# A hybrid diffusion block: norm statistics summed by a matrix of ones, and rsqrt over whole rows

## The chip, the cores and the metric

The kernel runs on one core of a Trainium2 chip. The metric is the time on the device of one execution, in microseconds; the time before is 2035.62 us, the median of three runs (2035.23 to 2038.11). The engines are TensorE (PE in the profile; PEld is its loading of weights), VectorE (DVE), ScalarE (ACT), GpSimd (POOL) and SyncE (SP), which issues the large loads.

## The reference, cut to what matters

Two streams of 256 tokens, latent and context, pass through two layers of width 1024. A layer is an FFN, a mixer of four branches, and a second FFN. Ahead of each stands an RMS norm with a scale and a shift per channel:

```
def rmsnorm(x, g):
    y = x * rsqrt(mean(x * x, axis=-1) + EPS)
    return y * g
h = rmsnorm(x, g) * (1 + mod[3 * slot + 1]) + mod[3 * slot]
x = x + 0.5 * mod[3 * slot + 2] * (silu(a) * b) @ w2      # FFN; the mixer is alike, with w_o
def layernorm(x, g, b):                                   # over 256 channels, in the conformer branch
    mu = mean(x); var = mean(square(x - mu))
    return (x - mu) * rsqrt(var + EPS) * g + b
```

The context stream ends with the second layer's keys and values, so from the second mixer on only the latent stream goes on. A last RMS norm stands at the end.

## The kernel before, in words

Activations lie with channels on the 128 partitions and tokens along the row: `xt` has eight tiles k of 128 channels, and 512 tokens, stream 0 in columns 0 to 255 and stream 1 in 256 to 511. Every main product is made of three matmuls, `mm3` (L215 to L217): the high and the low part of a weight times the high part of the input, and the high part of the weight times the low part of the input. A block of weights is loaded (`raw`), cast to `whi` on ScalarE (L199), and its rest `wlo` is made on VectorE (L200). Of `whi` and `wlo` there are six buffers each, of `raw` four; `spent` marks where a block's last matmul stands.

**The end of a stage.** `down` (called at the end of each FFN and mixer) makes the eight output tiles m. `residual` adds each to `xt` (L417, VectorE), and for the next norm its square is made on ScalarE (L409, or L406 for m = 0) and added to `acc` (L413). With two streams the last LAST = 2 tiles are made by stream: first the matmuls of stream 0 for both, over 256 columns, then `nxt.stat(0)`, then those of stream 1, `nxt.stat(1)`, then `nxt.apply(0)`. The next stage begins with `nxt.apply(1)` and a group of four units, whose matmuls over stream 0 run first, k by k through the four units, and then those over stream 1, unit by unit. This stands at four places: the first FFN, the first mixer, the second FFN and the third.

**The statistics.** `x_rstd(s)` sums squares over channels, which lie on partitions. `tok_stat` does it by matmuls that take `acc`, and the last tile's square apart, as weights and a column of ones as input (L258), one per 128 tokens; so the sums stand in a column, tokens on partitions. `rsqrt` is nine VectorE operations on 128x2 (L230 to L247). `tok_bcast` spreads the column over all partitions by transposes (L267) into PSUM (`aux`), from where `part` reads it: for each k a product z (L464, VectorE), the high part (L468, ScalarE) and the low part (L469, VectorE).

**The other users.** `conv` makes the layer norm of the conformer branch in the same way, once for the mean and once for the variance, over 512 tokens in the first mixer and 256 in the second; it is a generator, of which `tap` takes steps between matmuls. `LateNorm` serves the last FFN: the products are made without rstd, which is applied after them; its `late_stat` is called in the middle of the first group. `FinalNorm` is the last one.

**What sets the order.** Apart from the start of the kernel, the order on each engine is made by a planner that runs ahead of time: it takes the program's instructions, and picks for an engine among those that may run by their order in the program. Small tiles come from pools: tag s1 has HSLOT = 6 slots of 128x256 (the squares, z, the small DFT table of `fourier`, loaded at L811), tag s2 has 47 of 128x512, PSUM has four `mm` and four `aux`. A tile takes a slot where it is first written and gives it back after its last use.

Of the kernel before, what the change touches and what calls it, by code (L numbers as in the profile page):

```python
# [10 lines left out]
F32 = mybir.dt.float32  # L11
# [34 lines left out]
TAP_0 = (2, 1)  # L46
TAP_1 = (1, 3)

LAST = 2
HSLOT = 6  # L50
FREE = 2
NSLOT = 47
# [29 lines left out]
def hybrid_block(ctx: ExitStack, tc: tile.TileContext, a, out, dbg=None):  # L82
# [25 lines left out]
    def small(n, dt=F32, tag=None, bufs=6):  # L108
        return sm.tile([P, n], dt, tag=tag or f"sm{n}", name=nm("sm"), bufs=bufs)
# [30 lines left out]
    make_identity(nc, ident)  # L140
    ones_d = const.tile([P, 1], F32, name="ones_d")
    nc.vector.memset(ones_d, 1.0 / D)
    ones_c = const.tile([P, 1], F32, name="ones_c")
    nc.vector.memset(ones_c, 1.0 / 256)
    ones_w = const.tile([P, 63], F32, name="ones_w")
    nc.vector.memset(ones_w, 0.0)
    nc.vector.memset(ones_w[:, 31:32], 1.0)
# [13 lines left out]
    nc.scalar.activation(cw[:, :, 0:2], c_in, AF.Silu)  # L161


    ln_b_h = const.tile([P, DEPTH, 2], F32, name="ln_b_h")
    nc.gpsimd.tensor_scalar_mul(ln_b_h, ln_b, 0.5)
    dw_h = const.tile([P, DEPTH, 2, TAPS], F32, name="dw_h")
    nc.gpsimd.tensor_scalar_mul(dw_h, dw_w, 0.5)
    b_gate_h = const.tile([P, DEPTH, 4, KD], F32, name="b_gate_h")
    nc.gpsimd.tensor_scalar_mul(b_gate_h, b_gate, 0.5)

    rope_c = const.tile([P, S], F32, name="rope_c")
# [50 lines left out]
        nc.vector.tensor_tensor(out=lo[:, :n], in0=src, in1=hi[:, :n], op=ALU.subtract)  # L222
        return hi, lo

    def rsqrt(ps, n):

        h = small(n, tag=f"rh{n}")
        y = small(n, tag=f"rs{n}")
        t = small(n, tag=f"rt{n}")
        nc.vector.tensor_scalar(out=h, in0=ps, scalar1=0.5, scalar2=0.5 * EPS, op0=ALU.mult, op1=ALU.add)  # L230


        nc.vector.tensor_scalar(
            out=y.bitcast(I32), in0=h.bitcast(I32), scalar1=-0.5,
            scalar2=float(0x5F3759DF - 0x400000 - 2**31 + round(np.log2(RSQRT) * 2**23)), op0=ALU.mult, op1=ALU.add,
        )
        nc.vector.tensor_tensor(out=t, in0=y, in1=y, op=ALU.mult)
        nc.vector.tensor_tensor(out=t, in0=t, in1=h, op=ALU.mult)
        nc.vector.scalar_tensor_tensor(
            out=y, in0=t, scalar=1.5 * RSQRT**2, in1=y, op0=ALU.subtract, op1=ALU.mult  # L240
        )
        nc.vector.tensor_tensor(out=t, in0=y, in1=y, op=ALU.mult)
        nc.vector.tensor_tensor(out=t, in0=t, in1=h, op=ALU.mult)
        nc.vector.scalar_tensor_tensor(
            out=t, in0=t, scalar=5 / 3 * RSQRT**6, in1=t, op0=ALU.subtract, op1=ALU.mult
        )
        nc.vector.scalar_tensor_tensor(  # L247
            out=y, in0=t, scalar=1.25 * RSQRT**12, in1=y, op0=ALU.add, op1=ALU.mult
        )
        return y  # L250

    def tok_stat(srcs, ones, T):

# [10 lines left out]
    def tok_bcast(r, T):  # L264
        ps = paux()
        for j in range(T // P):
            nc.tensor.transpose(ps[:, j * P : (j + 1) * P], r[:, j : j + 1].to_broadcast([P, P]), ident)  # L267
        return ps
# [131 lines left out]

    last_square = {}

    def square_in(k, s):
        c = cols(s)
        if k == 0:
            nc.scalar.activation(acc[:, c], xt[:, k, c], AF.Square)  # L406
            return
        sq = s1()
        nc.scalar.activation(sq, xt[:, k, c], AF.Square)  # L409
        if k == KD - 1:  # L410
            last_square[s] = sq
            return
        nc.vector.tensor_tensor(out=acc[:, c], in0=acc[:, c], in1=sq, op=ALU.add)  # L413

    def residual(m, s, ps, G, sq):
        c = cols(s)
        nc.vector.scalar_tensor_tensor(  # L417
            out=xt[:, m, c], in0=ps[:, c], scalar=G[:, m, s : s + 1], in1=xt[:, m, c],
            op0=ALU.mult, op1=ALU.add,
        )  # L420
        if sq:
            square_in(m, s)

    def x_rstd(s, T=S):
        J = T // P
        ps = tok_stat([acc[:, s * S : s * S + T], last_square.pop(s)], ones_d, T)
        return tok_bcast(rsqrt(ps[:, :J], J), T)

    class Norm:

# [43 lines left out]
    class LateNorm(Norm):  # L474
# [6 lines left out]
            pass  # L481

        def late_stat(self):
            rstd = x_rstd(0)
            self.r = s2()
            nc.scalar.copy(self.r[:, :S], rstd[:, :S])

        def begin(self):
            Norm.begin(self)
# [73 lines left out]
    def down(blocks, parts, NB, G, last, nxt, group=1, filler=None):  # L563
# [12 lines left out]
        for g, count in starts:  # L576
# [12 lines left out]
            spent(*ws)  # L589
            for i, ps in enumerate(pss):  # L590
                for s in range(NB):
                    residual(g + i, s, ps, G, last)
                if last and NB == 1:
                    nxt.tile(g + i)
            if not last and filler:
# [76 lines left out]
    def mixer(l, NB, norm, nxt, filler):  # L672
# [75 lines left out]
        def conv():  # L748
# [14 lines left out]
                    )  # L763
                    yield

            J = T // P
            o = [keep.pop(("co", i)) for i in range(2)]
            tot = s2()
            nc.vector.tensor_tensor(out=tot[:, :T], in0=o[0][:, :T], in1=o[1][:, :T], op=ALU.add)
            yield  # L770
            ps = tok_stat([tot], ones_c, T)
            mu = small(J)
            nc.vector.tensor_copy(mu, ps[:, :J])
            yield
            mub = tok_bcast(mu, T)
            sq = []
            for i in range(2):
                nc.vector.tensor_tensor(out=o[i][:, :T], in0=o[i][:, :T], in1=mub[:, :T], op=ALU.subtract)
                q = s2()
                nc.scalar.activation(q[:, :T], o[i][:, :T], AF.Square)  # L780
                sq.append(q)
            nc.vector.tensor_tensor(out=sq[0][:, :T], in0=sq[0][:, :T], in1=sq[1][:, :T], op=ALU.add)
            yield
            ps = tok_stat([sq[0]], ones_c, T)
            r = rsqrt(ps[:, :J], J)
            yield
            rb = tok_bcast(r, T)
            for i in range(2):
                y, th = s2(), s2()
                nc.vector.scalar_tensor_tensor(  # L790
# [540 lines left out]
```

## Time and profile before

| | us |
|---|---|
| median of three runs | 2035.62 |
| the profiled execution | 2034.05 |
| its span | 2032.2 |
| PE busy | 1998.6 (98%) |
| DVE busy | 1325.8 (65%) |
| ACT busy | 731.9 (36%) |

The profile is of one execution; its span goes from the first to the last instruction of the program. Starts in a timeline are microseconds from the start of the span. Matmuls are pipelined: the time one takes on TensorE is the distance from its start to the next one's, and its length in the table is longer. A float32 matmul shows as two records. In square brackets stands the idle time of the engine ahead of a row, and what ended it.

### The profile page before, as it was taken

To read this page: it belongs to the slowest core of one execution; us is meant where nothing else is said; L and a number is where in the kernel's file an instruction comes from. 1 tells how busy PE (TensorE), PEld (TensorE's weight loads), DVE (VectorE), ACT (ScalarE), POOL (GpSimd) and SP (SyncE) were. 2 spreads that over 40 slices of the span, in tenths; PEclk is the share of its full clock that TensorE was granted. 3 is DMA by queue.
4 is the path that set the end of the run, shared out by engine and by line. 5 is a ranking of instruction groups with operands and counts; after the bars stand their busy time and mean duration, and the time that the engine had idled before them with its cause. 6 is when DMAs were issued, how large, how long until landed. Compare 5 with 4: busy or idle time off the path is not lost.

```text
span 2032.2 us, 28076 instructions
## 1 busy us (share of the span) xinstructions
PE 1998.6 (98%) x11074; PEld 1709.5 (84%) x11074; DVE 1325.8 (65%) x2338; ACT 731.9 (36%) x1142; POOL 5.1 (0%) x30
## 2 busy tenths in 40 slices
PE   6999999999999999999999999999999999999998
PEld 4888878888887778888888888888888999899998
DVE  5886697676756654689578455552424878777665
ACT  3322322333344442432222234222223545665443
POOL 0000000000000000000000000000000000000000
PEclk8999999999999999999999999999999999999999
DMA  7755466433221323266457432643333453446663
GB/s 284 243 177 188 149 207 188 148 96 99 73 83 57 109 73 94 74 206 200 150 179 241 152 125 85 197 139 90 112 88 102 145 161 120 140 152 201 182 182 94
DMA packets 83492, 294.08 MB, mean 145 GB/s; under 512 B 9504, under 2 KB 10144, under 8 KB 83360
## 3 DMA queue, kind: packets, MB, share of 16 engines
q1 hardware_dynamic: 82784, 291.54, 45.9%
q8 instruction: 87, 1.43, 0.3%
q10 hardware_dynamic: 576, 0.75, 0.1%
q14 instruction: 45, 0.37, 0.1%
HBM read 289.10 MB, written 1.05 MB: 143 GB/s over the span
## 4 chain that ended last, share of the span: by engine, by line
PE 96%; DVE 2%; ACT 1%; issue 0%; DMA 0%; DVEq 0%; ACTq 0%
PE mm L215 30%; PE mm L216 30%; PE mm L217 30%; PE aux L989 1%; PE aux L972 1%; PE aux L945 1%; PE aux L337 1%; PE aux L258 1%; PE aux L832 1%; PE aux L294 0%; PE aux L857 0%; PE aux L267 0%; PE aux L818 0%; DVE acc L1144 0%; DMA par<-in_par 0%
## 5 line engine op out<-in xcount | busy, mean ns | idle before, releaser
L215 PE MATMUL mm<-s,whi 128*128 128x512 f32 (+2 forms) x3354 | 1168.3, 349 | 2.3 <-ACT s L468 1.9
L216 PE MATMUL mm<-s,whi 128*128 128x512 f32 (+2 forms) x3354 | 1162.4, 347 | 2.1 <-DVE s L469 2.1
L217 PE MATMUL mm<-s,wlo 128*128 128x512 f32 (+2 forms) x3354 | 1162.3, 347 | 1.3 <-DVE wlo L200 1.3
L199 ACT CAST whi<-raw 128x1024 fp32r<-128x1024 f32 (+1 forms) x408 | 416.6, 1032 | 919.8 <-PE mm L216 698.5
L215 PEld LDWEIGHTS mm<-s,whi 128*128 128x128 f32 x3354 | 633.8, 189 | 96.3 <-issue 8.5
L217 PEld LDWEIGHTS mm<-s,wlo 128*128 128x128 f32 x3354 | 634.5, 189 | 80.4 <-DVE wlo L200 1.7
L216 PEld LDWEIGHTS mm<-s,whi 128*128 128x128 f32 x3354 | 635.0, 189 | 79.0 <-DVE s L469 3.1
L200 DVE TENSOR_TENSOR wlo<-raw,whi 128x1024 fp32r<-128x1024 f32 (+1 forms) x408 | 486.3, 1199 | 319.9 <-ACT whi L199 316.7
L358 DVE SCALAR_TENSOR_TENSOR s<-ada,cw,s 128x512 f32<-128x512 f32 x392 | 268.8, 745 | 48.2 <-DMA ada<-in_w_ada 48.0
L417 DVE SCALAR_TENSOR_TENSOR xt<-mm,modG,xt 128x256 f32<-128x256 f32 x192 | 84.5, 478 | 118.5 <-PE mm L217 118.0
L221 ACT CAST s<-s 128x512 fp32r<-128x512 f32 (+1 forms) x104 | 59.4, 571 | 85.4 <-DVE s L642 52.5
L760 DVE SCALAR_TENSOR_TENSOR s<-pad,dw_h,s 128x512 f32<-128x512 f32 (+1 forms) x120 | 73.8, 615 | 2.1
L222 DVE TENSOR_TENSOR s<-s,s 128x512 fp32r<-128x512 f32 (+1 forms) x104 | 64.8, 623 | 5.5 <-ACT s L221 5.5
L1060 ACT ACTIVATE s<-mm,b_gate_h 128x512 f32<-128x512 f32 (+1 forms) x64 | 35.4, 579 | 77.1 <-PE mm L217 76.7
L468 ACT ACTIVATE s<-s,mod 128x256 fp32r<-128x256 f32 x80 | 38.1, 504 | 37.9 <-DVE s L464 37.9
L1083 DVE SCALAR_TENSOR_TENSOR s<-s,mm 128x512 f32<-128x512 f32 x48 | 32.7, 682 | 27.6 <-PE mm L217 22.1
L642 DVE TENSOR_TENSOR s<-s,mm 128x512 f32<-128x512 f32 x66 | 44.9, 680 | 3.6 <-PE mm L217 3.5
L949 DVE TENSOR_REDUCE sm<-aux 128x1 f32<-128x512 f32 (+1 forms) x48 | 28.6, 595 | 26.3 <-PE aux L945 26.2
L957 ACT ACTIVATE s<-aux,sm,sm 128x512 f32<-128x512 f32 (+1 forms) x48 | 34.0, 708 | 29.2 <-DVE sm L952 29.2
L513 DVE TENSOR_TENSOR s<-mm,s 128x256 f32<-128x256 f32 x44 | 18.1, 420 | 36.2 <-PE mm L217 36.2
L632 ACT ACTIVATE s<-mm 128x512 f32<-128x512 f32 x66 | 38.9, 589 | 5.7 <-PE mm L217 5.7
L469 DVE SCALAR_TENSOR_TENSOR s<-s,mod,s 128x256 fp32r<-128x256 f32 x80 | 36.1, 478 | 1.5 <-ACT s L468 1.5
(134 smaller groups left out, 697.3 us busy)
## 6 DMA issues: line engine op xcount, KB each, us to landing
raw<-in_w SPq DMA_DIRECT2D x208, 512.0 KB, 4.4
ada<-in_w_ada SPq DMA_DIRECT2D x144, 512.0 KB, 3.9
raw<-in_w_in SPq DMA_DIRECT2D x100, 512.0 KB, 4.1
raw<-in_w SPq DMA_DIRECT2D x64, 448.0 KB, 4.0
raw<-in_w_br SPq DMA_DIRECT2D x20, 512.0 KB, 3.7
raw<-in_w_o SPq DMA_DIRECT2D x16, 512.0 KB, 4.4
xt<-in_xt SPq DMA_DIRECT2D x4, 512.0 KB, 6.1
s<-s SPq DMA_DIRECT2D x16, 128.0 KB, 2.2
```

The lines of the kernel that those rows point to most:

```text
L199: nc.scalar.copy(hi[:, :n], raw[:, :n]),
L200: nc.vector.tensor_tensor(out=lo[:, :n], in0=raw[:, :n], in1=hi[:, :n], op=ALU.subtract),
L215: nc.tensor.matmul(ps, lhsT=wh, rhs=xh, start=first, stop=False)
L216: nc.tensor.matmul(ps, lhsT=wh, rhs=xl, start=False, stop=False)
L217: nc.tensor.matmul(ps, lhsT=wl, rhs=xh, start=False, stop=last)
L221: nc.scalar.copy(hi[:, :n], src)
L222: nc.vector.tensor_tensor(out=lo[:, :n], in0=src, in1=hi[:, :n], op=ALU.subtract)
L358: nc.vector.scalar_tensor_tensor(out=t, in0=src, scalar=cs, in1=t, op0=ALU.mult, op1=ALU.add)
L417: nc.vector.scalar_tensor_tensor(out=xt[:, m, c], in0=ps[:, c], scalar=G[:, m, s : s + 1], in1=xt[:, m, c], op0=ALU.mult, op1=ALU.add,)
L632: nc.scalar.activation(s[:, :T], ps[:, :T], AF.Silu, bias=bias)
L642: nc.vector.tensor_tensor(out=h[:, :T], in0=s[:, :T], in1=ps[:, :T], op=ALU.mult)
L760: nc.vector.scalar_tensor_tensor(out=ov, in0=h[:, :NB, j : j + S], scalar=dw_h[:, l, i, j : j + 1], in1=ov, op0=ALU.mult, op1=ALU.add,)
```

## The change

Sums over partitions for the norms that are followed by another stage, and for the conformer's layer norm, are made by `sum_all`: one float32 matmul with a 128x128 matrix of 1 / D as weights and the squares (or values) as input, which leaves the sum in every partition. `rsqrt` then works on the whole 128x256 (128x512 in the first layer's conformer norm) instead of 128x2 or 128x4, and its result needs no spreading. Its scratch tiles h and t are taken from tag s1, the result y from a new tag `rstd` with two slots; in `conv` existing s2 tiles are used. The last tile's square is now added to `acc` like the others, save before the final norm, which keeps the old way. `LateNorm` uses the result without a copy. In `conv` the mean is subtracted with its factor in one operation, and the step for the copy of the mean is gone, so the generator has one step fewer. LAST becomes 3. `dw_w` and `b_gate` are halved in place, without tiles of their own.

```diff
--- before.py
+++ after.py
@@ -46,7 +46,7 @@
 TAP_0 = (2, 1)
 TAP_1 = (1, 3)
 
-LAST = 2
+LAST = 3
 HSLOT = 6
 FREE = 2
 NSLOT = 47
@@ -140,8 +140,8 @@
     make_identity(nc, ident)
     ones_d = const.tile([P, 1], F32, name="ones_d")
     nc.vector.memset(ones_d, 1.0 / D)
-    ones_c = const.tile([P, 1], F32, name="ones_c")
-    nc.vector.memset(ones_c, 1.0 / 256)
+    all_d = const.tile([P, P], F32, name="all_d")
+    nc.vector.memset(all_d, 1.0 / D)
     ones_w = const.tile([P, 63], F32, name="ones_w")
     nc.vector.memset(ones_w, 0.0)
     nc.vector.memset(ones_w[:, 31:32], 1.0)
@@ -161,11 +161,10 @@
     nc.scalar.activation(cw[:, :, 0:2], c_in, AF.Silu)
 
 
+    dw_h, b_gate_h = dw_w, b_gate
     ln_b_h = const.tile([P, DEPTH, 2], F32, name="ln_b_h")
     nc.gpsimd.tensor_scalar_mul(ln_b_h, ln_b, 0.5)
-    dw_h = const.tile([P, DEPTH, 2, TAPS], F32, name="dw_h")
     nc.gpsimd.tensor_scalar_mul(dw_h, dw_w, 0.5)
-    b_gate_h = const.tile([P, DEPTH, 4, KD], F32, name="b_gate_h")
     nc.gpsimd.tensor_scalar_mul(b_gate_h, b_gate, 0.5)
 
     rope_c = const.tile([P, S], F32, name="rope_c")
@@ -222,11 +221,9 @@
         nc.vector.tensor_tensor(out=lo[:, :n], in0=src, in1=hi[:, :n], op=ALU.subtract)
         return hi, lo
 
-    def rsqrt(ps, n):
-
-        h = small(n, tag=f"rh{n}")
-        y = small(n, tag=f"rs{n}")
-        t = small(n, tag=f"rt{n}")
+    def rsqrt(ps, n, tiles=None):
+
+        h, y, t = tiles or [small(n, tag=f"r{x}{n}", bufs=3) for x in "hst"]
         nc.vector.tensor_scalar(out=h, in0=ps, scalar1=0.5, scalar2=0.5 * EPS, op0=ALU.mult, op1=ALU.add)
 
 
@@ -248,6 +245,12 @@
             out=y, in0=t, scalar=1.25 * RSQRT**12, in1=y, op0=ALU.add, op1=ALU.mult
         )
         return y
+
+    def sum_all(src):
+
+        ps = paux()[:, : src.shape[-1]]
+        nc.tensor.matmul(ps, lhsT=all_d, rhs=src, start=True, stop=True)
+        return ps
 
     def tok_stat(srcs, ones, T):
 
@@ -400,31 +403,33 @@
 
     last_square = {}
 
-    def square_in(k, s):
+    def square_in(k, s, apart):
         c = cols(s)
         if k == 0:
             nc.scalar.activation(acc[:, c], xt[:, k, c], AF.Square)
             return
         sq = s1()
         nc.scalar.activation(sq, xt[:, k, c], AF.Square)
-        if k == KD - 1:
+        if apart and k == KD - 1:
             last_square[s] = sq
             return
         nc.vector.tensor_tensor(out=acc[:, c], in0=acc[:, c], in1=sq, op=ALU.add)
 
-    def residual(m, s, ps, G, sq):
+    def residual(m, s, ps, G, sq, apart=False):
         c = cols(s)
         nc.vector.scalar_tensor_tensor(
             out=xt[:, m, c], in0=ps[:, c], scalar=G[:, m, s : s + 1], in1=xt[:, m, c],
             op0=ALU.mult, op1=ALU.add,
         )
         if sq:
-            square_in(m, s)
-
-    def x_rstd(s, T=S):
-        J = T // P
-        ps = tok_stat([acc[:, s * S : s * S + T], last_square.pop(s)], ones_d, T)
-        return tok_bcast(rsqrt(ps[:, :J], J), T)
+            square_in(m, s, apart)
+
+    def x_rstd(s):
+        if s in last_square:
+            ps = tok_stat([acc[:, cols(s)], last_square.pop(s)], ones_d, S)
+            return tok_bcast(rsqrt(ps[:, :2], 2), S)
+        y = sp.tile([P, S], F32, tag="rstd", name=nm("rstd"), bufs=2)
+        return rsqrt(sum_all(acc[:, cols(s)]), S, (s1(), y, s1()))
 
     class Norm:
 
@@ -481,9 +486,7 @@
             pass
 
         def late_stat(self):
-            rstd = x_rstd(0)
-            self.r = s2()
-            nc.scalar.copy(self.r[:, :S], rstd[:, :S])
+            self.r = x_rstd(0)
 
         def begin(self):
             Norm.begin(self)
@@ -589,7 +592,7 @@
             spent(*ws)
             for i, ps in enumerate(pss):
                 for s in range(NB):
-                    residual(g + i, s, ps, G, last)
+                    residual(g + i, s, ps, G, last, isinstance(nxt, FinalNorm))
                 if last and NB == 1:
                     nxt.tile(g + i)
             if not last and filler:
@@ -763,28 +766,24 @@
                     )
                     yield
 
-            J = T // P
             o = [keep.pop(("co", i)) for i in range(2)]
             tot = s2()
             nc.vector.tensor_tensor(out=tot[:, :T], in0=o[0][:, :T], in1=o[1][:, :T], op=ALU.add)
             yield
-            ps = tok_stat([tot], ones_c, T)
-            mu = small(J)
-            nc.vector.tensor_copy(mu, ps[:, :J])
-            yield
-            mub = tok_bcast(mu, T)
+            mub = sum_all(tot[:, :T])
             sq = []
             for i in range(2):
-                nc.vector.tensor_tensor(out=o[i][:, :T], in0=o[i][:, :T], in1=mub[:, :T], op=ALU.subtract)
+                nc.vector.scalar_tensor_tensor(
+                    out=o[i][:, :T], in0=mub, scalar=-D / 256, in1=o[i][:, :T], op0=ALU.mult, op1=ALU.add
+                )
                 q = s2()
-                nc.scalar.activation(q[:, :T], o[i][:, :T], AF.Square)
+                nc.scalar.activation(q[:, :T], o[i][:, :T], AF.Square, scale=(D / 256) ** 0.5)
                 sq.append(q)
             nc.vector.tensor_tensor(out=sq[0][:, :T], in0=sq[0][:, :T], in1=sq[1][:, :T], op=ALU.add)
             yield
-            ps = tok_stat([sq[0]], ones_c, T)
-            r = rsqrt(ps[:, :J], J)
+            rb, t = s2(), tot
+            rsqrt(sum_all(sq[0][:, :T]), T, (sq[1][:, :T], rb[:, :T], t[:, :T]))
             yield
-            rb = tok_bcast(r, T)
             for i in range(2):
                 y, th = s2(), s2()
                 nc.vector.scalar_tensor_tensor(
```

## Rows read from the trace of the kernel before

**Rows 1.** The page, busy time, share and count, of TensorE.
```profile
PE 1998.6 (98%) x11074; PEld 1709.5 (84%) x11074; DVE 1325.8 (65%) x2338; ACT 731.9 (36%) x1142; POOL 5.1 (0%) x30
```

**Rows 2.** Timeline of PE, 394 to 402: start, length, line, tiles.
```profile
394.79 0.39 PE L215 MATMUL mm<-s,whi 128*128 128x512 f32 x1
...
396.83 0.28 PE L215 MATMUL mm<-s,whi 128*128 128x256 f32 x1
...
401.74 0.28 PE L217 MATMUL mm<-s,wlo 128*128 128x256 f32 x1
```

**Rows 3.** Timeline of all engines, 839 to 844, stream 0's statistics.
```profile
839.60 0.50 PE L258 MATMUL aux<-ones_d,acc 128*128 128x1 f32 x4
...
839.96 0.36 PE L215 MATMUL mm<-s,whi 128*128 128x256 f32 x1
...
843.44 0.19 PEld L267 LDWEIGHTS aux<-ident,sm 128*128 128x128 f32 x2 [0.26 <-DVE sm L247]
```

**Rows 4.** Timeline of PE behind E, 846 to 850.
```profile
846.72 0.50 PE L258 MATMUL aux<-ones_d,acc 128*128 128x1 f32 x4
...
848.21 0.61 PE L258 MATMUL aux<-ones_d,s 128*128 128x1 f32 x4 [0.99 <-ACT s L409]
...
848.68 0.72 PE L215 MATMUL mm<-s,whi 128*128 128x256 f32 x4
...
849.92 0.38 PE L216 MATMUL mm<-s,whi 128*128 128x256 f32 x1 [0.52 <-DVE s L469]
```

**Rows 5.** Timeline of VectorE (DVE), 844 to 848.
```profile
844.51 1.22 DVE L200 TENSOR_TENSOR wlo<-raw,whi 128x1024 fp32r<-128x1024 f32 x1
...
846.92 0.48 DVE L417 SCALAR_TENSOR_TENSOR xt<-mm,modG,xt 128x256 f32<-128x256 f32 x1 [0.84 <-PE mm L217]
...
847.32 0.86 DVE L464 SCALAR_TENSOR_TENSOR s<-xt,modA,aux 128x256 f32<-128x256 f32 x2
```

**Rows 6.** Timeline of ScalarE (ACT), 846 to 848.
```profile
846.79 1.04 ACT L199 CAST whi<-raw 128x1024 fp32r<-128x1024 f32 x1 [1.76 <-PE mm L216]
847.75 0.41 ACT L409 ACTIVATE s<-xt 128x256 f32<-128x256 f32 x1
```

**Rows 7.** Timeline of VectorE at the fourth stage end.
```profile
1588.00 0.17 DVE L392 TENSOR_SCALAR modG<-mod 128x16 f32<-128x16 f32 x1
1588.08 0.86 DVE L464 SCALAR_TENSOR_TENSOR s<-xt,modA,aux 128x256 f32<-128x256 f32 x2
```

**Rows 8.** Instructions of line 811: count, duration min/median/max, first and last start.
```profile
L811 SPq DMA_DIRECT2D s<-in_dft x2: 328/377/426, 419.8 to 1614.6; - x2
```

**Rows 9.** Groups by line and form on VectorE: count, busy us, mean ns.
```profile
L413 DVE TENSOR_TENSOR acc<-acc,s 128x256 f32<-128x256 f32 x60 | 23.4, 420 | 4.7 <-ACT s L409 4.7
...
L464 DVE SCALAR_TENSOR_TENSOR s<-xt,modA,aux 128x256 f32<-128x256 f32 x64 | 28.9, 472 | 0.0
...
L961 DVE TENSOR_SCALAR s<-s,sm 128x256 f32<-128x256 f32 x16 | 5.6, 351 | 0.4
```

**Rows 10.** Timeline of VectorE, three chained taps.
```profile
1639.96 1.52 DVE L760 SCALAR_TENSOR_TENSOR s<-pad,dw_h,s 128x256 f32<-128x256 f32 x3
```

**Rows 11.** Timeline of PE, float32 matmuls of 256 columns.
```profile
519.35 1.02 PE L818 MATMUL aux<-s,s 128*128 128x256 f32 x4
...
520.44 0.40 PE L216 MATMUL mm<-s,whi 128*128 128x512 f32 x1
```

**Rows 12.** Timeline of PE, first mean of the conformer's norm.
```profile
603.21 1.05 PE L258 MATMUL aux<-ones_c,s 128*128 128x1 f32 x8
```

**Rows 13.** Timeline of VectorE in the second mixer.
```profile
1723.53 0.43 DVE L801 SCALAR_TENSOR_TENSOR s<-s,s 128x256 fp32r<-128x256 f32 x1 [0.48 <-ACT s L800]
...
1731.16 0.68 DVE L1083 SCALAR_TENSOR_TENSOR s<-s,mm 128x512 f32<-128x512 f32 x1
```

**Rows 14.** Windows: length, busy us per engine, granted clock, DMA.
```profile
650.00:652.00 2.00, 0.51 (x3) 0.09 (x3) 1.45 (x4) 1.57 (x4) 0.00 (x0) 1.00 0.01 4
...
653.50:657.00 3.50, 3.50 (x16) 2.44 (x16) 2.95 (x10) 2.27 (x7) 0.00 (x0) 0.51 0.00 0
```

## The prediction

> **What bounds the kernel now.** Read the page first: PE is busy for 98% of the span [rows 1], and the chain that ended last runs over PE for nearly all of it, so the time is the sum of PE's matmuls and of the few places where PE has none to run. The timeline of PE gives the matmuls' own pace: over 512 columns one starts 0.227 us after the other (394.79 to 396.83, nine steps), over 256 columns 0.120 us (to 401.74, 41 steps) [rows 2]. What lies above that pace can be listed, and the change touches one kind of place in it: the end of a stage, where `down` finishes stream 0, then stream 1, and the next norm begins. There are four alike, near 408, 847, 1219 and 1587 us. I call E the end of stream 1's last matmul; in rows 3 to 6 E is 846.72.
>
> Before E the statistics of stream 0 stand among stream 1's matmuls: a group of L258 takes 0.36 us from its start to the next matmul (839.60 to 839.96), there are two such groups, and the transposes L267 come with a wait of 0.26 us for the last step of rsqrt, some 0.4 in all [rows 3]: 1.1 us. After E, PE waits 0.99 us for a square, then 0.52 us for the first low part of the new norm; L216 starts at 849.92, 3.20 us behind E, and only four main matmuls (0.48) ran before it [rows 4]: 2.7 us lost, and another pair of transposes later, about 0.2. So one stage end costs 4.0 us before the change.
>
> **What holds the first product of the next norm back.** This is the point on which I decide. L464 of stream 0 needs rstd of stream 0, whose transposes ran at 843.4 [rows 3]. Yet VectorE first takes a `wlo` for a much later block (844.51) and then L417 of stream 1 (846.92), and only behind that come the first two L464, at 847.32 [rows 5]. At the fourth stage end even a modG for the stage after next goes ahead (1588.00), and L464 follows (1588.08) [rows 7]. So it isn't the order of importance: L464 was not yet allowed. What it needs besides its inputs is a slot of tag s1, and the tile asked for just before it is the square of the last residual. A second witness: the load of the small DFT table needs no input and an s1 slot, and it is issued at 419.8 and 1614.6 [rows 8], behind each mixer's last norm products, and not in the hundreds of microseconds before. I read both as one rule of the planner: tiles of a tag are handed out in the order of the program.
>
> **The change part by part.** In the new `x_rstd` the scratch tiles h and t of rsqrt are s1 tiles, asked for in `stat(1)`, ahead of `apply(0)`. By the reading above the first L464 then waits until t of stream 1 is written first, which is the third step of rsqrt(1).
>
> Sizes of one step: a product over 128x256 lasts 0.42, one with a scalar as well 0.47, with scalars alone 0.35 [rows 9]; where a step needs the one before, add a gap: three chained taps take 1.52, so (1.52 - 0.48) / 2 = 0.52 from start to start [rows 10]. Nine steps are then about 4.2 us in place of nine of 0.2. Independent ones may start 0.39 apart (two L464 in 0.86) [rows 5].
>
> The price of `sum_all`: no such weights exist before; the nearest is L818, two float32 matmuls with 256 columns, which push the following main matmuls back by 1.09 - 0.23 = 0.86 us, 0.43 each [rows 11]. With 0.03 for the change of weights I take 0.46; below, 0.43; above, 0.6 if its result must drain first.
>
> After E then: L417 at E+0.20 and 0.48 long [rows 5]; the square at E+1.03, behind a cast that E releases [rows 6], done at E+1.45. The cast's `wlo` (1.2 us, as at 844.51 [rows 5]) is ready at E+1.1, when VectorE has nothing else; before the change it had L464s to do. I let it go first: the added `acc` step runs from E+2.3 to E+2.7, `sum_all` gives its result at E+3.3, steps 1 and 2 of rsqrt end at E+4.1, the third starts, and L464 follows at E+4.5. ScalarE's high part is ready at E+5.5, where L215 may run, and the low part comes behind two or three steps of rsqrt and two L464 at 0.35 to 0.39 each: L216 at about E+6.5. Four L215 ran before: 6.0 us lost, with `sum_all` in it, against 2.9. Without the `wlo` ahead it is E+5.7, 5.2 lost. From there each k takes VectorE about 1.5 us while rsqrt and the norm alternate, PE 12 x 0.12 = 1.44: no further loss.
>
> On the other side: before E one `sum_all` for two groups and two transposes, 0.46 for 1.1. A third tile split by stream: 21 matmuls over 512 columns become 42 over 256, 21 x (2 x 0.120 - 0.227) = 0.3 us (24 in the mixer, the same) [rows 2]; it keeps a third pair of whi and wlo until stream 1, so the fourth block of the next stage is cast and split some 5 us before E instead of earlier: hidden by stream 1's 7.5 us, at most 1.4 us (one k) if not. On SP's queue the loads keep their order, and GpSimd's two scalings run beside the first loads. Sum per stage end: -0.6 + 3.1 + 0.3 = +2.8, with bounds +1.9 (no `wlo` ahead) and +3.6 (`sum_all` at its upper price, one more step before the low part); four of them +11.2.
>
> VectorE's rows say that independent steps overlap, 0.39 from start to start at 0.47 length [rows 5]. The Trainium skill, "VectorE: DVE Perf Modes", section Terms, says that a flush follows each operation and the next can't issue until the pipe is empty. The measured rows decide; by the page the four or five steps ahead of the first low part would take 0.47 each, 0.4 us more per stage end and 1.6 us in all.
>
> The clock: PE was still for 1.49 us of 650 to 652, ran half of the time there, and then had a granted clock of 0.51 from 653.5 to 657, which is the 1.2 GHz level [rows 14]. After the change PE stands for some 2.7 us, does 0.46, and stands for 2.3. I expect such a stretch at each end. It costs half of the 3.4 us that PE could have used: between 0 (it falls on waiting) and 1.7; I take 0.85, times four +3.4.
>
> The conformer's layer norm and the late norm: in the first mixer two L258 groups of eight (each some 0.9 to the next matmul; one lasts 1.05 [rows 12]) and two groups of four transposes (twice a pair, 0.4 by estimate) are 2.6 us; two `sum_all` over 512 columns 1.7: -0.9. In the second mixer at half the width -0.25, in the late norm -0.6: -1.75. The longer rsqrt there (+2.5 us over 256 columns, about +4.5 over 512) is hidden: in the second mixer the norm's last step is at 1723.53 and the first result made from it is read at 1731.16 [rows 13], some 5 us of matmuls of the third gate lie between; without that cover +2.5. The LateNorm's rstd is wanted only when half a group of matmuls (5.8 us by 48 x 0.12) has run. Scaling dw_h and b_gate in place, a memset of 128 columns: beside the first loads, nothing; one `mu` copy and one ScalarE copy less, off the path.
>
> Sum: +11.2 + 3.4 - 1.75 = +12.8 on the profiled execution's 2034.05. That lies 1.57 under the median of the runs, 2035.62; against the median it is 2048.4.
>
> **Rivals.**
> 1. The tags are not handed out in order (or L464's wait has another cause, such as L417 itself): L464 starts right behind the last L417 as now. For it: in each case L464 does follow L417 at once. Against: rows 7 and 8. Then PE's restart stays at E+3.2, the groups and transposes go (-0.6 - 0.2), the split costs 0.3: -0.5 per end, -2.0, with -1.75 for the norms: 2031.9; as VectorE has slack or not, 2030 to 2033. Faster. It decides as soon as L464 stands ahead of rsqrt(1).
> 2. VectorE becomes the bound at the change of stream. Even if L464 starts early, behind E VectorE has 32 norm steps of 0.39, nine of rsqrt at 0.34 and a `wlo`, 12.5 + 3.1 + 1.2 + 0.9 = 17.7 us, while PE wants stream 1's last part near E + 3.2 + 11.5 + 2.5 = 17.2. That gives back 0.5 per end: 2033.9, no change.
> 3. L464 waits as forecast, but the clock holds and no `wlo` goes ahead: +1.9 x 4 - 1.75 = +5.9: 2041.5, the lower end of the forecast's own case.
>
> **How the numbers follow.** No change means within 0.2%, about what runs of this kernel can tell: 2031.5 to 2039.7. Forecast with rival 3: 0.68, from 2040 to 2056 (3.6 per end and 1.7 for the clock: +19.4). Rival 1: 0.18, about half of it beyond the bound, and with a VectorE that gains more than I see I leave 0.16 for faster. Rival 2 and mixtures: 0.14. Same 0.16, slower 0.68. Range 2031 to 2056.
>
> **What would show it.** In the timeline of VectorE after the change the first L464 of each of the four norms stands behind the third step of the second rsqrt; if it stands right behind the last L417, rival 1 is it. PE's first wait after E should be 2 to 3 us and the second about 2; the granted clock in the 10 us after E should show 0.5 for a stretch. `sum_all` should be two records of 0.21 us. The forecast is wrong if the four stage ends lose less than 5 us each.

## The result, and the profile after

The changed kernel takes 2051.34 us, the median of five runs (2049.73 to 2051.64), beside 2035.23 for the kernel before (five runs): a ratio of 1.0079, interval 1.0068 to 1.0091, so slower by 14 to 18.5 us. The forecast was 2048.4, in a range from 2031 to 2056. The profiled execution took 2049.73 against 2034.05: +15.7 us, where +12.8 was forecast.

The lines of the changed kernel stand up to five lower or higher than before: `mm3` is L214 to L216, the cast and its rest L198 and L199, `sum_all` L252, the steps of rsqrt L227 to L244, the acc step L416, the square L412, the residual L420, and the norm's product, high and low part L469, L473, L474.

The page first, busy time of each engine; the line that answers to [rows 1]:

```profile
PE 2001.6 (98%) x11061; PEld 1712.0 (84%) x11061; DVE 1354.9 (66%) x2345; ACT 734.0 (36%) x1141; POOL 5.1 (0%) x30
```

PE's busy time rose by 3.0 us only, and the span by 15.7. So it isn't work that was added, and the next place to look is what PE waited for. In the waits (engine, tile, line, what ended the wait; us in total, times, longest) these stand in the place of L258 for a square, 0.99 us at three of the four ends, and of L216 for a low part, 0.52 us at each [rows 4]:

```profile
PE mm L214 <- ACT s L473: 8.7, 5, 2.5
PE aux L252 <- DVE acc L416: 8.3, 4, 2.6
PE mm L214 <- ACT whi L198: 1.8, 1, 1.8
```

The first two are those of the four stage ends (one of the five for L473, 1.1 us, stands at the start of the kernel), and the third is for a cast, which the forecast did not have. The second end shows the first two in detail. E is 850.31 there. PE, behind the last matmul of stream 1 (answers to [rows 4]):

```profile
850.19 0.28 PE L216 MATMUL mm<-s,wlo 128*128 128x256 f32 x1
853.08 0.70 PE L252 MATMUL aux<-acc,all_d 128*128 128x256 f32 x2 [2.61 <-DVE acc L416]
856.02 1.22 PE L214 MATMUL mm<-s,whi 128*128 128x256 f32 x4 [2.24 <-ACT s L473]
857.05 0.48 PE L215 MATMUL mm<-s,whi 128*128 128x256 f32 x1
857.33 0.41 PE L216 MATMUL mm<-s,wlo 128*128 128x256 f32 x1
```

ScalarE, the cast that E releases and the square behind it (answers to [rows 6]):

```profile
850.39 1.04 ACT L198 CAST whi<-raw 128x1024 fp32r<-128x1024 f32 x1 [1.51 <-PE mm L215]
851.38 0.42 ACT L412 ACTIVATE s<-xt 128x256 f32<-128x256 f32 x1
855.46 0.51 ACT L473 ACTIVATE s<-s,mod 128x256 fp32r<-128x256 f32 x1 [3.67 <-DVE s L469]
```

VectorE (answers to [rows 5]):

```profile
850.80 0.48 DVE L420 SCALAR_TENSOR_TENSOR xt<-mm,modG,xt 128x256 f32<-128x256 f32 x1
851.47 1.22 DVE L199 TENSOR_TENSOR wlo<-raw,whi 128x1024 fp32r<-128x1024 f32 x1 [0.19 <-ACT whi L198]
852.61 0.42 DVE L416 TENSOR_TENSOR acc<-acc,s 128x256 f32<-128x256 f32 x1
853.82 0.42 DVE L227 TENSOR_SCALAR s<-aux 128x256 f32<-128x256 f32 x1 [0.79 <-PE aux L252]
854.28 0.29 DVE L230 TENSOR_SCALAR rstd<-s 128x256 int32<-128x256 int32 x1
854.61 0.43 DVE L234 TENSOR_TENSOR s<-rstd 128x256 f32<-128x256 f32 x1
854.95 0.48 DVE L469 SCALAR_TENSOR_TENSOR s<-xt,modA,rstd 128x256 f32<-128x256 f32 x1
...
856.41 0.48 DVE L474 SCALAR_TENSOR_TENSOR s<-s,mod,s 128x256 fp32r<-128x256 f32 x1
```

Read it from the top. The square is done at 851.80, but VectorE has taken a `wlo` at 851.47 and does the acc step at 852.61; `sum_all` follows. The result starts rsqrt at 853.82, and only behind its third step, L234, does the first product of stream 0 appear, for which everything but a slot was there long before. The windows of PE (length, busy us and instructions of PE, PEld, DVE, ACT, POOL, granted clock, DMA share and GB/s) show what came next, the clock at its lower level for 6.8 us:

```profile
854.80:861.60 6.80, 5.58 (x27) 5.58 (x28) 6.80 (x19) 3.05 (x6) 0.00 (x0) 0.53 0.15 61
861.60:865.00 3.40, 3.40 (x31) 3.40 (x30) 3.40 (x10) 2.04 (x4) 0.00 (x0) 1.00 0.00 0
```

From E to the 96th main matmul behind it, counted in the trace, it was 14.4 us at all four ends before; now it is 19.0, 19.5, 17.7 and 19.7.

### The profile page after: what moved, and what is told of

It reads as the page before. It is cut to its first block, busy times and chain, and to the rows that moved or that the text cites. A ratio compares the mean times of both kernels' runs of the same rounds, so it can differ in the third digit from the quotient of the medians.

```text
span 2047.9 us, 28048 instructions
## 1 busy us (share of the span) xinstructions
PE 2001.6 (98%) x11061; PEld 1712.0 (84%) x11061; DVE 1354.9 (66%) x2345; ACT 734.0 (36%) x1141; POOL 5.1 (0%) x30
## 4 chain that ended last, share of the span: by engine, by line
PE 92%; DVE 4%; DMA 1%; ACT 1%; issue 1%; DVEq 0%; ACTq 0%; SPq 0%
PE mm L214 29%; PE mm L215 29%; PE mm L216 29%; PE aux L988 1%; DVE wlo L199 1%; PE aux L971 1%; PE aux L944 1%; PE aux L340 1%; DMA ada<-in_w_ada 1%; PE aux L831 1%; PE aux L297 0%; DVE s L361 0%; PE aux L252 0%; ACT whi L198 0%; DMA raw<-in_w_br 0%
## 5 line engine op out<-in xcount | busy, mean ns | idle before, releaser
L214 PE MATMUL mm<-s,whi 128*128 128x512 f32 (+2 forms) x3383 | 1175.8, 349 | 11.1 <-ACT s L473 8.7
L215 PE MATMUL mm<-s,whi 128*128 128x512 f32 (+2 forms) x3383 | 1172.0, 347 | 0.3 <-DVE s L474 0.2
L216 PE MATMUL mm<-s,wlo 128*128 128x512 f32 (+2 forms) x3383 | 1170.5, 347 | 1.6 <-DVE wlo L199 1.6
L198 ACT CAST whi<-raw 128x1024 fp32r<-128x1024 f32 (+1 forms) x408 | 416.9, 1033 | 911.0 <-PE mm L215 686.0
L214 PEld LDWEIGHTS mm<-s,whi 128*128 128x128 f32 x3383 | 642.7, 191 | 107.7 <-ACT s L473 13.3
L216 PEld LDWEIGHTS mm<-s,wlo 128*128 128x128 f32 x3383 | 644.3, 191 | 79.4 <-DVE wlo L199 2.0
L215 PEld LDWEIGHTS mm<-s,whi 128*128 128x128 f32 x3383 | 644.7, 191 | 76.4 <-DVE s L474 0.9
L199 DVE TENSOR_TENSOR wlo<-raw,whi 128x1024 fp32r<-128x1024 f32 (+1 forms) x408 | 486.7, 1200 | 319.3 <-ACT whi L198 316.6
L420 DVE SCALAR_TENSOR_TENSOR xt<-mm,modG,xt 128x256 f32<-128x256 f32 x192 | 84.8, 479 | 111.9 <-PE mm L216 111.9
L763 DVE SCALAR_TENSOR_TENSOR s<-pad,par,s 128x512 f32<-128x512 f32 (+1 forms) x120 | 73.8, 615 | 2.1
L1059 ACT ACTIVATE s<-mm,par 128x512 f32<-128x512 f32 (+1 forms) x64 | 35.4, 581 | 69.2 <-PE mm L216 69.2
L473 ACT ACTIVATE s<-s,mod 128x256 fp32r<-128x256 f32 x80 | 39.8, 508 | 54.6 <-DVE s L469 54.6
L516 DVE TENSOR_TENSOR s<-mm,rstd 128x256 f32<-128x256 f32 x44 | 18.1, 420 | 33.1 <-PE mm L216 33.1
L412 ACT ACTIVATE s<-xt 128x256 f32<-128x256 f32 x70 | 27.2, 411 | 34.5 <-DVE xt L420 34.4
```

The source lines that it names most:

```text
L198: nc.scalar.copy(hi[:, :n], raw[:, :n]),
L199: nc.vector.tensor_tensor(out=lo[:, :n], in0=raw[:, :n], in1=hi[:, :n], op=ALU.subtract),
L214: nc.tensor.matmul(ps, lhsT=wh, rhs=xh, start=first, stop=False)
L215: nc.tensor.matmul(ps, lhsT=wh, rhs=xl, start=False, stop=False)
L216: nc.tensor.matmul(ps, lhsT=wl, rhs=xh, start=False, stop=last)
L420: nc.vector.scalar_tensor_tensor(out=xt[:, m, c], in0=ps[:, c], scalar=G[:, m, s : s + 1], in1=xt[:, m, c], op0=ALU.mult, op1=ALU.add,)
```

## The experiments

Theory A is the forecast's: slots of tag s1, handed out in program order, hold the first product back. Theory B: VectorE's wide steps as such are what PE waits for, whatever the slots. Each kernel ran in five rounds beside the kernel before, whose median was 2033.2 to 2034.3 there; a tenth of a per cent is 2.03 us.

### Slots: h and t in a tag of their own

```diff
-        return rsqrt(sum_all(acc[:, cols(s)]), S, (s1(), y, s1()))
+        return rsqrt(sum_all(acc[:, cols(s)]), S, (own(), y, own()))   # tag "own", 2 slots; NSLOT = 46
```

> The changed kernel, with h and t of the wide rsqrt taken from a tag of their own (two slots; tag s2 has one slot fewer). Nothing else is different. Theory A (the order in which slots of tag s1 are handed out holds the first product of the next norm behind the third step of the second rsqrt): the first product stands right behind the last residual or the last acc step, PE's second wait after E shrinks from 2.2 to 2.5 us to below 1, the granted clock at the stage ends stays at 1.0 or falls once or twice instead of four times, and the time is 2032 to 2039. Theory B (VectorE's wide steps as such, nine of 0.4 us per stream among the products, are what PE waits for): moving two tiles changes nothing, PE still restarts 5 us after E, 2046 to 2052. In between, 2040 to 2045, both have a part, and the distance from E to the 24th matmul says how much.

Measured: 2039.95, ratio 1.0029 (1.0020 to 1.0038). Against the change's 1.0079, two tiles in another tag give back 10 of 16 us: theory A holds for most of it, though the time lies just above what it was given, and so do PE's waits for the first high part, up to 1.8 us where I had put below 1. The clock fell at two ends, as expected. What is left stands in the trace at the third end, PE and then VectorE (`sum_all` is L255 here, the acc step L419, the product L472):

```profile
1224.29 1.22 PE L255 MATMUL aux<-acc,all_d 128*128 128x256 f32 x2 [2.19 <-DVE acc L419]
```
```profile
1222.69 1.21 DVE L202 TENSOR_TENSOR wlo<-raw,whi 128x1024 fp32r<-128x1024 f32 x1
1223.82 0.41 DVE L419 TENSOR_TENSOR acc<-acc,s 128x256 f32<-128x256 f32 x1
1224.16 0.87 DVE L472 SCALAR_TENSOR_TENSOR s<-xt,modA,rstd 128x256 f32<-128x256 f32 x2
1225.55 0.42 DVE L230 TENSOR_SCALAR own<-aux 128x256 f32<-128x256 f32 x1 [0.52 <-PE aux L255]
```

The products now stand ahead of the second rsqrt. But the squares' own s1 slots still go ahead of them, the `wlo` and the acc step as well, and PE's order has `sum_all` ahead of the next stage. Not all that is left stands at the ends: the first mixer, taken between two main matmuls that are the same in both programs, takes 3.0 us more than in the kernel before, with a wait of 2.48 for a cast and one of 2.05 for a softmax step.

### Slots: z in a tag of its own, in both kernels

```diff
-                z = s1()
+                z = zt()          # tag "z", 3 slots; HSLOT = 3, so the bytes stay
```

> The kernel before the change, with the products z (L464) in a tag of their own: three slots for z, three left for s1, the same bytes. Theory A (slots of a tag are handed out in the program's order, and z stands in line behind stream 1's squares): with a line of its own the first z runs before the last residual of stream 1, PE's wait for the first low part goes, 1 to 2.5 us per end: 2024 to 2030. If L464's place has another cause, nothing moves: 2032 to 2036.

> The changed kernel with z in a tag of its own (three slots; three left for s1, from which h and t of rsqrt still come). Theory A: as with h and t in their own tag, and better, since z also passes the squares: first products before E, PE's wait after E below 1 us, 2026 to 2034. Theory B (VectorE's wide steps are what PE waits for): rsqrt of stream 1 then alternates with the products of stream 0, PE waits at the change of stream instead, 2038 to 2044.

Measured: before_z 2031.01, ratio 0.9985 (0.9976 to 0.9994); after_z 2030.52, ratio 0.9980 (0.9972 to 0.9989). The second is the cleanest evidence for theory A: the computation of the change is untouched, its statistics as wide as ever, and all 16 us come back and some 4 more, so that it is faster than the kernel before. At the third end PE, where E is 1217.21:

```profile
1217.09 0.28 PE L219 MATMUL mm<-s,wlo 128*128 128x256 f32 x1
1219.10 0.51 PE L217 MATMUL mm<-s,whi 128*128 128x256 f32 x2 [1.73 <-ACT s L476]
1219.44 0.59 PE L255 MATMUL aux<-acc,all_d 128*128 128x256 f32 x2
1219.69 0.47 PE L218 MATMUL mm<-s,whi 128*128 128x256 f32 x1
```

One wait of 1.73, L218 at E+2.5 in place of E+6.7, and `sum_all` where it hurts nobody. This wait is longer than the expectation had it, which was below 1 us. Theory B's alternation of rsqrt and products is there, but PE doesn't catch up: the wait at the change of stream that it asked for stands at the second end alone, with 0.38 us.

before_z gained less than it was given. Its ends are 1.5 to 1.9 us shorter each, 7.3 in all, by the time from the 100th main matmul ahead of E to the 192nd behind it; but 5.7 us are lost again in the first mixer, where PE shows:

```profile
589.02 1.06 PE L340 MATMUL aux<-s,ones_w 128*32 128x512 f32 x6
592.30 1.03 PE L975 MATMUL aux<-ident,s 128*128 128x128 f32 x4 [2.22 <-DVE sm L963]
```

L340 (L337 before) are the later modulations' sums, eight matmuls that the kernel before did at 408.7, inside PE's wait at the first end. Without that wait they move on to 579 and 589, and there the softmax is late and the clock falls for 3.4 us. A wait that is closed had held work that now stands elsewhere.

### Order: apply(0) straight after stat(0)

```diff
                 nxt.stat(s)
-            nxt.apply(0)
+                if s == 0:
+                    nxt.apply(0)
```

> The changed kernel, with the next norm's apply(0) called straight after stat(0), ahead of stream 1's residuals in the program; its tiles stay in tag s1. Theory A: the products of stream 0 are then first in line for their slots, run while PE is still in stream 1, and PE goes on at E with no wait at all: 10 of the 11 us and the clock's 3 come back, and the 2.7 us that each end lost before the change too; 2022 to 2032, faster than before the change. Theory B: behind E VectorE still has nine wide steps and 16 products and low parts of stream 1 for PE's next 12 us, so PE is caught up at the change of stream: 2034 to 2042.

> The kernel before the change, with apply(0) straight after stat(0) and nothing else. Theory A: L464 of stream 0 runs before E there too, so most of the 2.7 us lost behind each E goes (all but the wait for the last square, if the statistics' matmuls stand ahead of the main ones): 1.5 to 2.7 us per end, 2024 to 2030. If L464's place behind the last residual had another cause than the slots of its tag, the order in the program changes nothing: 2034 to 2037.

Measured: after_early 2031.24, ratio 0.9988 (0.9979 to 0.9997); before_early 2031.35, ratio 0.9987 (0.9978 to 0.9996). With the program's order changed the slots' order changes, and 18 us of the change's price are gone, as theory A has it. These two runs by themselves can't tell the slots from the planner's preference for the program's order, which they change as well; own_tag and the runs with z apart leave that order alone, and they decide. Of the ends' old 2.7 us less comes back than I expected. In after_early theory B has its part: PE runs on at E, and stands at the change of stream, 10 us later:

```profile
860.85 0.74 PE L214 MATMUL mm<-s,whi 128*128 128x256 f32 x4 [1.55 <-ACT s L473]
```

There are three such waits, 4.5 us in all and none at the fourth end, where the wide rsqrt of stream 1 starts behind the steps of stream 0's norm and three `wlo`, and ends only then. In before_early it is the first mixer again: 7.2 us gained at the ends, 4.3 lost behind the same softmax wait of 2.22.

### LAST, the acc step and the clock

```diff
-LAST = 3                                        # after_last2
+LAST = 2
```

> The changed kernel with LAST = 2, two tiles by stream instead of three. The prediction gave the third tile +0.3 us per end, 1.2 in all: 2049 to 2051 if that holds and nothing else hangs on it. Rival: with three tiles stream 1's stretch is longer and gives the first rsqrt its cover; with two the first rsqrt reaches into the time behind E and the time goes up by 1 to 2 us per end: 2055 to 2059.

Measured: 2050.12, ratio 1.0078 (1.0065 to 1.0092), against 1.0079: the third tile moves nothing that can be measured. PE's waits for the acc step are longer with two tiles, 10.0 us in place of 8.3; that is about what the split of a third tile costs.

```diff
-        nc.tensor.matmul(ps, lhsT=all_d, rhs=src, start=True, stop=True)           # after_apart
+        for i, src in enumerate(srcs):          # acc, and the last square apart
+            nc.tensor.matmul(ps, lhsT=all_d, rhs=src, start=i == 0, stop=i == len(srcs) - 1)
...
```

> The changed kernel without the added acc step: the last square is summed by a second matmul into the same PSUM bank, as the kernel before did it with its column of ones. One float32 matmul more per stream (0.43 us each by the two records of 0.21), but the sum no longer waits for the acc step and the wlo ahead of it: the result comes at E + 2.0 in place of E + 3.3. Theory: 1.3 us less wait and 0.9 us more work per end, and a shorter stillness of PE, with or without the clock's fall: 2044 to 2050. If the acc step and the wlo cost nothing, the added matmuls show: 2052 to 2054.

Measured: 2047.95, ratio 1.0068 (1.0054 to 1.0081). The interval overlaps that of the change, so the 2 us are not settled by times; the trace at the second end shows the mechanism, the wait for a square of 0.90 where it was 2.61 for the acc step, and one more `sum_all`:

```profile
851.44 0.59 PE L253 MATMUL aux<-acc,all_d 128*128 128x256 f32 x2
852.93 0.70 PE L253 MATMUL aux<-s,all_d 128*128 128x256 f32 x2 [0.90 <-ACT s L413]
855.94 0.79 PE L214 MATMUL mm<-s,whi 128*128 128x256 f32 x2 [2.30 <-ACT s L474]
```

```diff
+            if s == 1: fill(xt[:, KD - 1, cols(1)], 4)      # after_busy, in Norm.stat
             self.rstd[s] = x_rstd(s)
+            if s == 1: fill(acc[:, cols(1)], 4)              # n matmuls with all_d, result unused
...
```

> The changed kernel with PE kept busy while it waits: at each stage end four float32 matmuls of 256 columns on the last tile of xt ahead of stream 1's sum, and four more on acc behind it, 1.7 us each lot, written to PSUM and never read. No wait is shorter by them, and up to 0.4 us each may be added. Theory K (some 5 us of the change's price is the clock that falls at the stage ends because PE stands): the granted clock stays at 1.0 at the ends, and the time falls by 3 to 5 us in spite of the added work: 2045 to 2048. If the clock's fall costs little, 2050 to 2054.

Measured: 2045.66, ratio 1.0062 (1.0048 to 1.0076): 3.5 us less than the change, with some 14 us of useless matmuls added (32 of 0.46). The intervals overlap a little, so here too the trace has to show it. At the second end, where E is 848.59:

```profile
849.61 1.99 PE L437 MATMUL aux<-xt,all_d 128*128 128x256 f32 x8 [0.87 <-DVE xt L420]
851.44 0.62 PE L252 MATMUL aux<-acc,all_d 128*128 128x256 f32 x2
851.89 1.89 PE L437 MATMUL aux<-acc,all_d 128*128 128x256 f32 x8
854.30 0.74 PE L214 MATMUL mm<-s,whi 128*128 128x256 f32 x4 [0.52 <-ACT s L482]
855.22 0.39 PE L215 MATMUL mm<-s,whi 128*128 128x256 f32 x1 [0.18 <-DVE s L483]
```

L214 starts at E+5.7 and L215 at E+6.6, as in the change; what PE waits for came hardly earlier. Yet the granted clock never left 1.0 at any of the four ends, and the 24th main matmul starts at E+9.0 in place of E+10.9. Nearly all of these 1.9 us are the clock's price by itself at that end. At the third end, where the clock cost the change nothing, the same matmul is 1.0 us later, for the added work.

### The conformer's norm

```diff
-            ps = tok_stat([tot], ones_c, T)     # norms_only: this part of the change on the kernel before
+            mub = sum_all(tot[:, :T])
...
```

> The kernel before the change with the conformer's layer norm of the change alone (two sums by the matrix of ones, rsqrt over the whole width); the norms between the stages stay as they were, LAST = 2. The prediction's term: -0.9 in the first mixer and -0.25 in the second, 1.15 faster, with the longer rsqrt hidden. Rival: the norm's result is wanted when it is made, and the wide rsqrt (some 4 us longer over 512 columns) comes back in part as a wait of PE in a mixer: 0 to +3.

Measured: 2038.05, ratio 1.0018 (1.0009 to 1.0027): slower by 2 to 5.5 us, the wrong way for the prediction's term; the middle of it, 3.7, lies beyond even the rival's 3. In the first mixer, VectorE's last step of the wide rsqrt and the softmax's reduction behind it (L949), then PE:

```profile
615.54 0.69 DVE L245 SCALAR_TENSOR_TENSOR s<-s,s 128x512 f32<-128x512 f32 x1
616.24 0.69 DVE L949 TENSOR_REDUCE sm<-aux 128x1 f32<-128x512 f32 x1
```
```profile
627.74 0.50 PE L215 MATMUL mm<-s,whi 128*128 128x512 f32 x1 [1.84 <-ACT whi L199]
```

The rsqrt runs on VectorE from 608.41 to 616.23, with three other steps between its nine. Then the norm and a softmax share VectorE and ScalarE: both halves' tanh and the exponents of the softmax stand ahead of a cast on ScalarE, which starts at 626.66 where before it was 624.08, and PE wanted its `whi` at 625.9. The clock falls behind that wait. The same wait of 1.8 for a `whi` stands in the waits of the change, above. A part of the 3.7 us is the clock at two stage ends, whose waits are those of before (last section).

```diff
-            mub = sum_all(tot[:, :T])           # after_oldconv, after_z_oldconv: conv as before
+            ps = tok_stat([tot], ones_c, T)
...
```

> The changed kernel with the conformer's layer norm as it was before the change (column of ones, narrow rsqrt, transposes); the norms between the stages as changed. Theory C (the conformer's wide rsqrt costs what it cost alone: VectorE is taken for 7.8 us, tanh and softmax slip past a cast on ScalarE, PE waits 1.8 us for whi in the first mixer, and the clock falls once in each mixer): 2 to 4 us come back, 2046 to 2049. The prediction's own term (-1.15 for the changed norm): 2051 to 2053.

> The changed kernel with z in a tag of its own and the conformer's layer norm as before the change: the two parts that cost something taken out, the wide statistics between the stages kept. By theories A and C 2 to 4 us below the run with z alone: 2026.5 to 2029. If the conformer's price there was only a place where the clock happened to fall: 2030 to 2032.

> The kernel before the change, narrow statistics throughout, with z in a tag of its own and LAST = 3, the rest of the change left out. If the wide statistics are worth something once nothing waits for slots, this stays behind the run above: 2030 to 2033. If they are worth nothing, and the third tile's cover helps the narrow ones too: 2026 to 2029.

Measured: after_oldconv 2048.46, ratio 1.0073 (1.0061 to 1.0086); after_z_oldconv 2027.85, ratio 0.9972 (0.9963 to 0.9981); before_z_last3 2032.05, ratio 0.9995 (0.9986 to 1.0004). The old norm in the conformer gives 1.2 us with the change's slots and 1.6 with z apart, each within the intervals; the `whi` wait is gone from both traces. With norms_only the sign is settled (the wide norm costs), the size isn't: 1 to 4 us.

after_z_oldconv beats both kernels, by 0.19% to 0.37% under the kernel before. That it also beats before_z_last3 does not show that wide statistics are better, as my expectation had it: at the four ends before_z_last3 is ahead by 0.9, -0.2, 0.9 and 0.7 us, and it loses 5.6 against the other in the first mixer, with the sums that moved there, the softmax wait of 2.2 and the clock. What the wide statistics are worth in themselves stays open.

## Why the prediction was right

- **L464 held back by the slots' order**: right. The first product stands right behind the third step of rsqrt(1) at all four ends (step and product: 411.43 and 411.77, 854.61 and 854.95, 1231.70 and 1232.04, 1601.50 and 1601.85); own_tag and after_z each move it by the slots alone.
- **The times behind E**: forecast residual E+0.2, square 1.03, `wlo` 1.1, acc step 2.3, result 3.3, L464 4.5, L215 5.5, L216 6.5. Measured at the second end: 0.49, 1.07, 1.16, 2.30, 3.51, 4.64, 5.71, 6.74 (for the first and second of `mm3`'s lines, now L214 and L215). The `wlo` did go ahead, and with the acc step it costs time: after_apart, whose second matmul reads the last square and waits for neither `wlo` nor acc step, has L214 at E+4.50 there. Where the forecast asked for waits of 2 to 3 us and about 2, the first end has 1.19 and 2.50 and the third 2.19 and 0.38, because eight matmuls of the modulations' sums (L340) run inside one of the two.
- **The ends in sum**: behind E the four lose 4.6, 5.1, 3.3 and 5.3 us up to the 96th main matmul, 18.3 in all. By the forecast's own count, the start of L215 behind E less the four matmuls ahead of it, it is 6.0 to 6.3 at each, where 6.0 was forecast. Main matmuls at half pace take 0.213 us each (857.33 to 861.17) in place of 0.120; what such matmuls lie above 0.120 sums to 6.1 us where it was 1.1 before, so the clock costs 5.1. The rest is 13.2, 3.1 to 3.4 per end, where 4 x 3.1 = 12.4 was forecast.
- **The clock**: right in kind, mis-sized in the sum: 3.4 forecast, 5.1 measured. It cost 1.4 to 2.0 at three ends and nothing at the third, where it fell on waiting and on the modulations' sums (work that stood at 1267 before; the way from the third end to the fourth is 1.2 us shorter without it). The Trainium skill, "TensorE: Matmul & The Clock Gate", section "A second HAM failure mode: psum-queue depth-cycling", tells of a kernel whose matmul groups leave small pauses, so that the clock goes up and down between its two levels and throughput falls. Here the trace agrees in kind: two waits of 2.6 and 2.2 us, and 0.53 behind them.
- **Price of `sum_all`**: 0.46 taken, with 0.03 in it for a change of weights that no run shows by itself; 0.35 measured when it stands alone among main matmuls (842.70 to 843.05; it is two records, of which four matmuls in a row take 0.46 each, 849.61 to 851.44 in after_busy). What it replaces was over-read: a group of L258 takes 0.37 and the transposes with their wait 0.24 from matmul to matmul, 0.98 in place of 1.1, for the 0.26 of rows 3 is idle time of the weight load. So the saving before E is 0.63 where 0.6 was forecast, and less the third tile the trace shows 0.4 at each end.

```profile
842.70 0.70 PE L252 MATMUL aux<-acc,all_d 128*128 128x256 f32 x2
843.05 0.47 PE L215 MATMUL mm<-s,whi 128*128 128x256 f32 x1
```

- **The third tile**, +1.2: without it the time is the same; a shorter wait for the acc step pays it back.
- **The conformer and late norms**, -1.75: the step that failed. The matmuls saved are more than worked out: by the distance to the next matmul 1.4 us in the first mixer, 0.5 in the second and 0.8 in the late norm, where 0.9, 0.25 and 0.6 stood. But "the longer rsqrt there is hidden" was judged by when the norm's result is read in the second mixer; in the first mixer it isn't the norm that is late but the softmax and a cast that share VectorE and ScalarE with it. In the trace of the change the first mixer, between the same main matmuls, takes 0.35 us longer than before, and what follows the 192nd main matmul behind the fourth end 0.17: +0.5 in place of -1.75. The clock is in these numbers: the kernel before has a stretch of 3.4 us at the lower level in the first mixer (653.5) and the change has one in the second (1752.1) instead.

So the total was near for two reasons. The largest term was right, and by luck the other errors in part cancel: the waits at the ends (+0.8), the clock (+1.7), the conformer and late norms (+2.3), the gain before E (-0.3), and the first 500 main matmuls (-1.45), in a profile that lacks the 10.2 us of low clock at the start of the kernel that the profile of before has; whether this is the cause is not shown. They leave the some 3 us by which the forecast was low; the other stretches of the kernel nearly cancel.

One reading of rows 14 is off, though nothing in the sum rests on it: PE was busy for 0.51 of those 2.00 us, a quarter and not half.

Rival 1 is ruled out by the first product's place, and both conditions of rival 3 failed: the clock fell and the `wlo` went ahead. Rival 2, a wait at the change of stream, appeared at more than one end only in after_early.

## What to carry to other kernels

Before a wide scratch tile is taken from a shared pool, look at which instructions get the next slots of that tag: a tile that is written late holds all that ask after it, and the profile then names a data producer, not the slot. Look at what runs inside a wait before closing it, and judge the cover of a longer step by every instruction that shares its engine, not by its own consumer alone.

## What the runs showed of the hardware that was not expected

Equal waits don't have equal clocks. At the second end norms_only has the waits of the kernel before (1.0 for the square and 0.5 for the low part), and the granted clock of the same stretch differs; norms_only first, then the kernel before:

```profile
850.90:854.30 3.40, 3.40 (x18) 3.40 (x18) 3.40 (x14) 1.85 (x5) 0.00 (x0) 0.54 0.00 0
```
```profile
850.90:854.30 3.40, 3.40 (x31) 3.40 (x31) 3.40 (x13) 1.89 (x4) 0.00 (x0) 1.00 0.00 0
```

Such a stretch costs about 1.5 us (here 6.99 from E to the 24th main matmul where the kernel before has 5.57), and the profiles of these kernels have between none and five, apart from the start and the last microseconds. So a difference of a few microseconds between two single executions can be the clock alone, and only trace rows or many runs tell. On VectorE, wide steps of which none needs the one before start 0.33 to 0.40 us apart at 0.42 to 0.48 length, and dependent ones 0.46. In after_early the nine steps of one rsqrt stand in a row, here the first and the last; they took 3.95 us, for which the forecast had 4.2:

```profile
855.78 0.41 DVE L227 TENSOR_SCALAR s<-aux 128x256 f32<-128x256 f32 x1
...
859.31 0.42 DVE L244 SCALAR_TENSOR_TENSOR rstd<-s,rstd 128x256 f32<-128x256 f32 x1
```
